# Output projection of a hybrid diffusion layer: the split of the activations moves one instruction ahead on ScalarE, and the last-but-one tile is normalised on VectorE

## The chip, the cores and the metric

The program runs on one core of a Trainium2 chip. The metric is the device time of one execution in microseconds (us). Engines are named as in the profile: PE is TensorE (PEld its weight loads), DVE is VectorE, ACT is ScalarE, POOL is GpSimd, and SP is the queue from which this kernel issues its transfers.

## The reference, cut to what matters

The kernel computes one layer for 2048 latent tokens and 128 context tokens. Three branches (a gated convolution, a gated spatial unit, windowed attention) give a concatenated activation of 1024 channels for each token. The change lies behind that, in the output projection and the closing normalisation:

```
out = jnp.concatenate([ya, yb, yc], axis=-1) @ w_out_l
x_new = _layernorm(ALPHA * x + gate[:, None] * out) * ln_g_l + ln_b_l
```

`_layernorm` subtracts the mean over the 1024 channels and divides by the root of the variance plus 1e-5.

## The kernel before

The branches write their activations, channels first, into a DRAM scratch `y_d`. The last stage reads them back in 17 tiles of 128 tokens (16 of the latent tokens, then the one of the context tokens) and runs one loop over these tiles, `for i in range(NT)`. There is no planner in this stage: every engine takes its instructions in the order in which the code is written.

For a tile, the following happens.

- SP loads the activations of the tile into `yf` (`out_load`, 512 KB, two buffers) and the residual input into `xr` (`x_again`, three buffers).
- The activations are split into a rounded part and a rest: ACT copies `yf` to `yh[:, 0]` (L1128), DVE subtracts that from `yf` and writes `yh[:, 1]` (L1129). Both are in `out_split`. The weights were split in the same way earlier.
- PE makes the tile's 1024 output columns in two halves of 512, each in a PSUM tile `ps` (three buffers), with 24 matmuls a half: 8 blocks of 128 channels by 3 products (rounded by rounded, rounded by rest, rest by rounded). The tile's `yh` is the weight that is loaded, so of a tile's 48 matmuls the first two need only the copy, and the third needs the subtraction too.
- DVE takes each half out of PSUM: times the gate (L1322), plus ALPHA times the residual (L1323), statistics (L1325). Behind the second half come the joined statistics (L1327) and a chain of instructions on single columns, L1329 to L1342, which makes the reciprocal root. This text calls it the chain.
- ACT then normalises the tile in place (L1343), POOL multiplies by `gam` (L1344) and adds `bet` (L1345), and SP stores the tile one iteration later (L1352).

In the code, `out_split` of tile i+1 stands at the head of iteration i. On ACT, therefore, the copy of a tile follows the normalisation of the tile two before it; on DVE the subtraction of a tile follows the chain of the tile two before it. The last tile (context) is made in three pieces of 512, 256 and 256 columns, and its normalisation is shared out among ACT, POOL and DVE (L1332 to L1350).

Of the kernel before, what the change touches and what calls it, by code (L numbers as in the profile page):

```python
# [11 lines left out]
F32 = mybir.dt.float32  # L12
F32R = mybir.dt.float32r
# [3 lines left out]
AF = mybir.ActivationFunctionType  # L17
ALU = mybir.AluOpType
# [4 lines left out]
P = 128  # L23
# [5 lines left out]
NT = TOK // P  # L29
# [67 lines left out]
    out_split=3100.0,  # L97
# [38 lines left out]
def hybrid_step(ctx: ExitStack, tc: tile.TileContext, x_prompt, x_sample, cache_k, cache_v, c, c_ctx,  # L136
# [3 lines left out]
    V, S, G, PE, SP = nc.vector, nc.scalar, nc.gpsimd, nc.tensor, nc.sync  # L140

    def open_pool(name, bufs=1, **kw):
        g = tc.tile_pool(name=name, bufs=bufs, **kw)
        return g, g.__enter__()
# [179 lines left out]
    for ks in VH:  # L324
        SP.dma_start(out=wB["v"]["st"][:, ks],
                     in_=w_in[0, ks.start * P:ks.stop * P, V0:V0 + 256].rearrange("(k p) f -> p k f", p=P))
# [16 lines left out]
    for g in range(4):  # L343
        SP.dma_start(out=bsb[64 * (g % 2):64 * (g % 2) + 64, g // 2, :],
                     in_=b_sp[0, g:g + 1, :].broadcast_to([64, P]))
# [774 lines left out]
    yhs, xts = {}, {}  # L1120

    def out_load(i):
        yhs[i] = outp["op"].tile([P, 8, P], F32, name="yf", bufs=2)
        SP.dma_start(out=yhs[i], in_=y_d[:, :, i * P:(i + 1) * P].rearrange("f p t -> p f t"))

    def out_split(i, yh):
        yf = yhs[i]
        S.activation(out=yh[:, 0], in_=yf, func=AF.Copy)  # L1128
        V.tensor_tensor(out=yh[:, 1], in0=yf, in1=yh[:, 0].bitcast(F32), op=ALU.subtract)  # L1129
        yhs[i] = yh  # L1130
# [20 lines left out]
    while cidx < len(jobs):  # L1151
# [37 lines left out]
        for ti, (t0, n) in enumerate(TILES):  # L1189
# [19 lines left out]
            if kind == "q":  # L1209
                for u in range(4 * ti, min(4 * ti + 4, 17)):  # L1210
# [4 lines left out]
                                       in1=QS[0:64, 0, t0:t0 + n], op0=ALU.mult, op1=ALU.subtract)  # L1215
                V.scalar_tensor_tensor(out=QS[0:64, 1, t0:t0 + n], in0=ps[64:128], scalar=cq[64:128],
                                       in1=QS[64:128, 1, t0:t0 + n], op0=ALU.mult, op1=ALU.subtract)
            elif kind == "k":
                for h in range(2):
# [3 lines left out]
                                           op0=ALU.mult, op1=ALU.subtract)  # L1223
                rng = {1: (0, 1024), 3: (1024, 2048)}.get(ti)
                if ti == 0:
                    cps = aps.tile([P, P], F32, name="cps", tag="o")
                    PE.transpose(cps, ckt, ident)
                    for h in range(2):
# [3 lines left out]
                                               op0=ALU.mult, op1=ALU.subtract)  # L1232
# [13 lines left out]
                if rng:  # L1246
                    r = slice(*rng)
# [37 lines left out]
    og2, o2 = open_pool("outl", side="left")  # L1285

    def x_again(i):
        xts[i] = o2.tile([P, D], F32, name="xr", bufs=3)
        SP.dma_start(out=xts[i], in_=src_rows(i))

    x_again(0)
    gam = o2.tile([P, D], F32, name="gam")
    bet = o2.tile([P, D], F32, name="bet")
# [5 lines left out]
    SP.dma_start(out=gam, in_=ln_g[0:1, :].broadcast_to([P, D]))  # L1299
    SP.dma_start(out=bet, in_=ln_b[0:1, :].broadcast_to([P, D]))  # L1300
    rs = {}
    for i in range(NT):
        if i + 1 < NT:
            out_split(i + 1, o2.tile([P, 2, 8, P], F32R, name="yh", bufs=2))
            x_again(i + 1)
        if i + 2 < NT:
            out_load(i + 2)
        yh, xt = yhs.pop(i), xts.pop(i)
        r = o2.tile([P, D], F32, name="r", bufs=3)
        last = i == NT - 1  # L1310
        cuts, sw = ((0, 512, 768, D), 256) if last else ((0, 512, D), 512)
        st = o2.tile([P, 8, 6], F32, name="ost", bufs=2)
        gt = gts[0 if i < NT - 1 else 1]
        for f0, f1 in zip(cuts, cuts[1:]):
            ps = aps.tile([P, 512], F32, name="ps", tag="pj", bufs=PJ)
            ps = ps[:, :f1 - f0]
            for k in range(KB):
                for q, (a, b) in enumerate(((0, 0), (0, 1), (1, 0))):
                    PE.matmul(out=ps, lhsT=yh[:, a, k, :], rhs=wo[:, b, k, f0:f1],  # L1319
                              start=(k == 0 and q == 0), stop=(k == KB - 1 and q == 2))  # L1320
            a = slice(f0, f1)
            V.tensor_tensor(out=r[:, a], in0=ps, in1=gt[:, a], op=ALU.mult)  # L1322
            V.scalar_tensor_tensor(out=r[:, a], in0=xt[:, a], scalar=ALPHA, in1=r[:, a], op0=ALU.mult, op1=ALU.add)  # L1323
            for b in range(f0, f1, sw):
                V.bn_stats(out=st[:, b // sw, :], in_=r[:, b:b + sw])  # L1325
        mv = o2.tile([P, 6], F32, name="omv", bufs=2)
        V.bn_aggr(out=mv[:, 0:2], in_=st[:, 0:D // sw])  # L1327
        v, y, t = mv[:, 1:2], mv[:, 2:3], mv[:, 3:4]
        V.tensor_scalar(out=v, in0=v, scalar1=EPS, scalar2=None, op0=ALU.add)  # L1329
        if last:  # L1330
            cut, mid = T["cut"], T["mid"]
            V.tensor_scalar(out=mv[:, 4:5], in0=mv[:, 0:1], scalar1=-1.0, scalar2=None, op0=ALU.mult)  # L1332
            S.activation(out=r[:, cut:], in_=r[:, cut:], func=AF.Identity, bias=mv[:, 4:5])
            G.tensor_tensor(out=r[:, cut:], in0=r[:, cut:], in1=gam[:, cut:], op=ALU.mult)
        V.tensor_scalar(out=t.bitcast(I32), in0=v.bitcast(I32), scalar1=1, scalar2=None, op0=ALU.logical_shift_right)  # L1335
        V.tensor_scalar(out=y.bitcast(I32), in0=t.bitcast(I32), scalar1=-1, scalar2=0x5F3759DF, op0=ALU.mult, op1=ALU.add)  # L1336
        for three in (3.0, 12.0, 768.0):
            V.scalar_tensor_tensor(out=t, in0=y, scalar=v, in1=y, op0=ALU.mult, op1=ALU.mult)  # L1338
            V.scalar_tensor_tensor(out=y, in0=t, scalar=three, in1=y, op0=ALU.subtract, op1=ALU.mult)  # L1339
        V.tensor_scalar(out=y, in0=y, scalar1=-1.0 / 8192, scalar2=None, op0=ALU.mult)  # L1340
        if not last:
            V.tensor_scalar(out=mv[:, 4:5], in0=mv[:, 0:1], scalar1=y, scalar2=-1.0, op0=ALU.mult, op1=ALU.mult)  # L1342
            S.activation(out=r, in_=r, func=AF.Identity, scale=y, bias=mv[:, 4:5])  # L1343
            G.tensor_tensor(out=r, in0=r, in1=gam, op=ALU.mult)  # L1344
            G.tensor_tensor(out=r, in0=r, in1=bet, op=ALU.add)  # L1345
        else:
            S.activation(out=r[:, mid:], in_=r[:, mid:], func=AF.Copy, scale=y)
            G.tensor_tensor(out=r[:, mid:], in0=r[:, mid:], in1=bet[:, mid:], op=ALU.add)
            V.scalar_tensor_tensor(out=r[:, :cut], in0=r[:, :cut], scalar=mv[:, 0:1], in1=gam[:, :cut], op0=ALU.subtract, op1=ALU.mult)  # L1349
            V.scalar_tensor_tensor(out=r[:, :mid], in0=r[:, :mid], scalar=y, in1=bet[:, :mid], op0=ALU.mult, op1=ALU.add)  # L1350
        if i > 0:
            SP.dma_start(out=y_sample[0, (i - 1) * P:i * P, :], in_=rs.pop(i - 1))  # L1352
        rs[i] = r
    r = rs.pop(NT - 1)
# [35 lines left out]
```

## Time and profile before

| | |
|---|---|
| median of 3 runs | 1187.61 us (1185.17 to 1192.42) |
| profiled execution, its own time | 1188.24 us |
| its span, first to last instruction | 1186.2 us |
| PE busy | 1069.7 us (90%) |
| DVE busy | 843.5 us (71%) |
| ACT busy | 447.3 us (38%) |
| POOL busy | 346.2 us (29%) |
| the last stage, from its first matmul to the end of the span | 958.6 to 1186.2 us |

The profiled execution lies 0.6 us above the median, so sums made against its 1188.24 us can be read against the median as they stand. 2.04 us of it lie outside the span. Shares of busy time are means over the whole program; what bounds the last stage is read from that stage alone.

### The profile page before, as it was taken

To read this page: it belongs to the slowest core of one execution; us is meant where nothing else is said; L and a number is where in the kernel's file an instruction comes from. 1 tells how busy PE (TensorE), PEld (TensorE's weight loads), DVE (VectorE), ACT (ScalarE), POOL (GpSimd) and SP (SyncE) were. 2 spreads that over 40 slices of the span, in tenths; PEclk is the share of its full clock that TensorE was granted. 3 is DMA by queue.
4 is the path that set the end of the run, shared out by engine and by line. 5 is a ranking of instruction groups with operands and counts; after the bars stand their busy time and mean duration, and the time that the engine had idled before them with its cause. 6 is when DMAs were issued, how large, how long until landed. Compare 5 with 4: busy or idle time off the path is not lost. (4 is left out here: it accounts for less than half of the span.)

```text
span 1186.2 us, 21036 instructions
## 1 busy us (share of the span) xinstructions
PE 1069.7 (90%) x8044; PEld 681.4 (57%) x8044; DVE 843.5 (71%) x2071; ACT 447.3 (38%) x758; POOL 346.2 (29%) x346
## 2 busy tenths in 40 slices
PE   5588989889968999999999999999988999888885
PEld 1377866477754455554545445545544477776774
DVE  4678866665562389954898549973899658777877
ACT  1432322223332266543655436753666321121111
POOL 0145655200002122102662022300325414334434
PEclk9699999989988999999999999999999999999998
DMA  9713104168957238754666746757476663433341
GB/s 330 260 43 103 59 10 142 54 211 294 308 185 197 77 74 147 130 127 102 113 145 122 152 105 125 150 125 150 97 136 119 198 211 107 144 123 106 120 129 54
DMA packets 254356, 165.50 MB, mean 140 GB/s; under 512 B 163600, under 2 KB 224808, under 8 KB 254256
## 3 DMA queue, kind: packets, MB, share of 16 engines
q1 hardware_dynamic: 254256, 164.16, 53.6%
q8 instruction: 63, 1.03, 0.4%
q14 instruction: 37, 0.30, 0.1%
HBM read 88.06 MB, written 36.21 MB: 105 GB/s over the span
## 5 line engine op out<-in xcount | busy, mean ns | idle before, releaser
L548 PE MATMUL pj<-h_hi,wring 128*128 128x512 f16 (+1 forms) x1280 | 336.2, 349 | 9.2 <-DMA wring<-wj_d 9.2
L548 PEld LDWEIGHTS <-wring 128*128 128x128 f16 x2400 | 211.7, 98 | 224.1 <-DMA wring<-wj_d 9.3
L548 PE MATMUL pj<-h_lo,wring 128*128 128x512 f16 (+1 forms) x640 | 217.9, 349 | 0.0
L1319 PE MATMUL ps<-wo,yh 128*128 128x512 f32 (+1 forms) x840 | 193.5, 390 | 21.0 <-DVE yh L1129 21.0
L1319 PEld LDWEIGHTS ps<-wo,yh 128*128 128x128 f32 x840 | 153.8, 188 | 60.5 <-DVE yh L1129 27.0
L1062 DVE SCALAR_TENSOR_TENSOR PH<-pt,sm,PH 128x608 f16<-128x608 f32 (+3 forms) x136 | 155.3, 1142 | 2.6 <-ACT PH L1059 2.4
L1002 POOL TENSOR_TENSOR TB<-raw,msk 128x480 f32<-128x480 f32 (+2 forms) x96 | 96.2, 1010 | 187.6 <-DVE sm L1043 187.6
L1059 ACT ACTIVATE PH<-pt,sm 128x608 f16<-128x608 f32 (+3 forms) x136 | 99.9, 734 | 95.1 <-ACT pt L1052 62.3
L1052 ACT ACTIVATE pt<-pt,sm,scal 128x608 f32<-128x608 f32 (+2 forms) x128 | 108.3, 846 | 57.6 <-DVE sm L1048 54.0
L1043 DVE CUSTOM_DVE_ANT_0 pt<-s,TB 128x608 f32<-128x608 f32 (+2 forms) x128 | 93.3, 729 | 11.2 <-PE s L1031 10.0
L558 PE MATMUL vvps<-wV,h_hi 128*128 128x256 f16 x544 | 94.0, 277 | 3.6 <-DVE vt L923 3.6
L558 PEld LDWEIGHTS <-h_hi 128*128 128x128 f16 x816 | 82.0, 102 | 23.1 <-issue 11.1
L548 PE MATMUL p<-h_hi,wring 128*128 128x512 f16 (+1 forms) x320 | 85.9, 352 | 1.9 <-DVE th L565 1.9
L1343 ACT ACTIVATE r<-r,omv 128x1024 f32<-128x1024 f32 x16 | 19.9, 1244 | 177.0 <-issue 141.1
L548 PEld LDWEIGHTS <-wB 128*128 128x128 f16 x768 | 63.4, 98 | 24.7 <-issue 1.3
L558 PE MATMUL vvps<-wV,h_lo 128*128 128x256 f16 x272 | 75.3, 277 | 0.0
L1344 POOL TENSOR_TENSOR r<-r,gam 128x1024 f32<-128x1024 f32 x16 | 38.2, 2388 | 126.4 <-ACT r L1343 126.4
L548 PE MATMUL ups<-h_hi,wB 128*128 128x128 f16 (+2 forms) x448 | 70.8, 267 | 0.3 <-DVE wB L238 0.3
L986 POOL TENSOR_SCALAR raw<-raw,scal 128x528 f32<-128x528 f32 x8 | 5.5, 704 | 220.2 <-DVE scal L189 165.8
L1129 DVE TENSOR_TENSOR yh<-yf,yh 128x1024 fp32r<-128x1024 f32 x17 | 41.0, 2410 | 35.2 <-ACT yh L1128 35.2
L1222 DVE SCALAR_TENSOR_TENSOR KL<-pj,scal,KH 64x512 f16<-64x512 f32 (+1 forms) x40 | 26.8, 670 | 54.1 <-ACT KH L1221 53.9
L496 POOL TENSOR_TENSOR h_lo<-hf,h_hi 128x512 f16<-128x512 f32 x34 | 39.9, 1179 | 74.9 <-DMA bsb<-in_b_spatial_dram 42.2
(214 smaller groups left out, 1712.0 us busy)
## 6 DMA issues: line engine op xcount, KB each, us to landing
wa<-in_w_ada_dram SPq DMA_DIRECT2D x24, 512.0 KB, 7.4
wraw<-in_w_in_dram SPq DMA_DIRECT2D x20, 512.0 KB, 5.7
wj_d<-wsp SPq DMA_DIRECT2D x40, 256.0 KB, 6.3
wring<-wj_d SPq DMA_DIRECT2D x20, 512.0 KB, 5.7
yf<-y_d SPq DMA_DIRECT2D x17, 512.0 KB, 5.6
xt<-in_x_sample_dram SPq DMA_DIRECT2D x16, 512.0 KB, 5.0
VW<-v_d SPq DMA_DIRECT2D x64, 128.0 KB, 5.1
xr<-in_x_sample_dram SPq DMA_DIRECT2D x16, 512.0 KB, 4.1
```

Of the source, the lines that this page charges most:

```text
L496: G.tensor_tensor(out=h_lo[:, k0:k0 + g, t0:t0 + n], in0=hv, in1=hi, op=ALU.subtract)
L548: PE.matmul(out=ps, lhsT=w(a, k) if callable(w) else w[:, a, k, :], rhs=mov(b, k), start=(k == 0 and i == 0), stop=(k == KB - 1 and i == 2))
L558: PE.matmul(out=ps, lhsT=a[:, k, i * P:(i + 1) * P], rhs=w[:, b, k, :], start=(k == 0 and q == 0), stop=(k == KB - 1 and q == 2))
L1002: G.tensor_tensor(out=TB[:, tslot(u) + h, P:P + n], in0=raws[h][:, off:off + n], in1=msk[:, mo:mo + n], op=ALU.add)
L1043: V.tensor_tensor_reduce(out=pt[:, :w], in0=src, in1=TB[:, tslot(u) + h, 0:w], op0=ALU.add, op1=ALU.max, scale=1.0, scalar=-3e38, accum_ou ...
L1052: S.activation(out=pt[:, :w], in_=src, func=AF.Exp, bias=sm[:, 1:2], scale=st_["isig"], accum_out=sm[:, 2:3])
L1059: S.activation(out=pb[:, 0:w], in_=pt[:, :w], func=AF.Copy, scale=sm[:, 3:4])
L1062: V.scalar_tensor_tensor(out=pb[:, wp:wp + w], in0=pt[:, :w], scalar=sm[:, 3:4], in1=pb[:, 0:w], op0=ALU.mult, op1=ALU.subtract)
L1129: V.tensor_tensor(out=yh[:, 1], in0=yf, in1=yh[:, 0].bitcast(F32), op=ALU.subtract)
L1222: V.scalar_tensor_tensor(out=KL[a, h, t0:t0 + n], in0=ps[a], scalar=ckk[a], in1=KH[a, h, t0:t0 + n], op0=ALU.mult, op1=ALU.subtract)
L1319: PE.matmul(out=ps, lhsT=yh[:, a, k, :], rhs=wo[:, b, k, f0:f1], start=(k == 0 and q == 0), stop=(k == KB - 1 and q == 2))
L1344: G.tensor_tensor(out=r, in0=r, in1=gam, op=ALU.mult)
```

## The change

Four things are done.

- `out_split` no longer runs inside the loop. Its two instructions become `yh_copy` and `yh_sub`. In iteration i, the copy of tile i+2 is issued on ACT ahead of the normalisation of tile i, and the subtraction of tile i+2 on DVE behind the chain of tile i.
- `yh` gets three buffers in place of two.
- The load of the activations is issued behind the subtraction, three tiles ahead, and so stands on SP in front of the store in place of behind it.
- Tile 15 (the last-but-one) is normalised by two DVE instructions of 1024 columns, in place of L1342, the ACT pass and the two POOL passes.

```
     rs = {}
+
+    def yh_copy(i):
+        if i < NT:
+            yh = o2.tile([P, 2, 8, P], F32R, name="yh", bufs=3)
+            S.activation(out=yh[:, 0], in_=yhs[i], func=AF.Copy)
+            yhs[i] = yhs[i], yh
+
+    def yh_sub(i):
+        if i < NT:
+            yf, yh = yhs[i]
+            V.tensor_tensor(out=yh[:, 1], in0=yf, in1=yh[:, 0].bitcast(F32), op=ALU.subtract)
+            yhs[i] = yh
+        if i + 1 < NT:
+            out_load(i + 1)
+
+    yh_copy(1)
+    yh_sub(1)
     for i in range(NT):
         if i + 1 < NT:
-            out_split(i + 1, o2.tile([P, 2, 8, P], F32R, name="yh", bufs=2))
             x_again(i + 1)
-        if i + 2 < NT:
-            out_load(i + 2)
         yh, xt = yhs.pop(i), xts.pop(i)
...
             a = slice(f0, f1)
+            if f0 == 0:
+                yh_copy(i + 2)
             V.tensor_tensor(out=r[:, a], in0=ps, in1=gt[:, a], op=ALU.mult)
...
-        if not last:
+        if i == NT - 2:
+            V.scalar_tensor_tensor(out=r, in0=r, scalar=mv[:, 0:1], in1=gam, op0=ALU.subtract, op1=ALU.mult)
+            V.scalar_tensor_tensor(out=r, in0=r, scalar=y, in1=bet, op0=ALU.mult, op1=ALU.add)
+        elif not last:
...
+        yh_sub(i + 2)
         if i > 0:
             SP.dma_start(out=y_sample[0, (i - 1) * P:i * P, :], in_=rs.pop(i - 1))
```

On ACT, early in the loop, the kernel before issues these (`r_11543`, `r_11625` and `r_11707` are tiles 1 to 3 under normalisation; `yh_11536` to `yh_11782` the split tiles 2 to 5):

```order
L1128 ACTIVATE yh_11536<-yf_11460 128x1024
L1343 ACTIVATE r_11543<-r_11543,omv_11601 128x1024
L1128 ACTIVATE yh_11618<-yf_11541 128x1024
L1343 ACTIVATE r_11625<-r_11625,omv_11683 128x1024
L1128 ACTIVATE yh_11700<-yf_11623 128x1024
L1343 ACTIVATE r_11707<-r_11707,omv_11765 128x1024
L1128 ACTIVATE yh_11782<-yf_11705 128x1024
```

The changed kernel issues these there (the same three tiles `r`; `yh_11489` to `yh_11734` are tiles 2 to 5):

```order
L1306 ACTIVATE yh_11489<-yf_11458 128x1024
L1362 ACTIVATE r_11462<-r_11462,omv_11522 128x1024
L1306 ACTIVATE yh_11570<-yf_11539 128x1024
L1362 ACTIVATE r_11543<-r_11543,omv_11603 128x1024
L1306 ACTIVATE yh_11652<-yf_11620 128x1024
L1362 ACTIVATE r_11625<-r_11625,omv_11685 128x1024
L1306 ACTIVATE yh_11734<-yf_11702 128x1024
L1362 ACTIVATE r_11707<-r_11707,omv_11767 128x1024
```

The copy of tile 5 stood behind the normalisation of tile 3 (`r_11707`) and now stands in front of it.

On DVE, at the boundary behind the chain of tile 3, the kernel before issues these (`omv` holds the single columns of the chain, `yh_11782` is tile 5, `r_11789` tile 4):

```order
L1340 TENSOR_SCALAR omv_11765<-omv_11765 128x1
L1342 TENSOR_SCALAR omv_11765<-omv_11765 128x1
L1129 TENSOR_TENSOR yh_11782<-yf_11705,yh_11782 128x1024
L1322 TENSOR_TENSOR r_11789<-ps_11791,gt0_11449 128x512
L1323 SCALAR_TENSOR_TENSOR r_11789<-xr_11703,r_11789 128x512
```

The changed kernel issues these there (`yh_11734` is tile 5):

```order
L1356 TENSOR_SCALAR omv_11767<-omv_11767 128x1
L1361 TENSOR_SCALAR omv_11767<-omv_11767 128x1
L1312 TENSOR_TENSOR yh_11734<-yf_11702,yh_11734 128x1024
L1338 TENSOR_TENSOR r_11789<-ps_11791,gt0_11449 128x512
L1339 SCALAR_TENSOR_TENSOR r_11789<-xr_11705,r_11789 128x512
```

Nothing moved on DVE here: the subtraction of tile 5 stood behind the chain of tile 3 already, since the head of one iteration and the end of the iteration before it are the same place.

At the end of the program DVE issues these in the changed kernel, behind the chain of tile 15 (`r_12689`) and ahead of the last tile (`r_12762`):

```order
L1356 TENSOR_SCALAR omv_12747<-omv_12747 128x1
L1358 SCALAR_TENSOR_TENSOR r_12689<-r_12689,omv_12747,gam_11447 128x1024
L1359 SCALAR_TENSOR_TENSOR r_12689<-r_12689,omv_12747,bet_11448 128x1024
L1338 TENSOR_TENSOR r_12762<-ps_12764,gt1_11451 128x512
L1339 SCALAR_TENSOR_TENSOR r_12762<-xr_12687,r_12762 128x512
```

The two instructions on 1024 columns are new on DVE; in the kernel before L1342 stood in their place.

## Rows read from the trace of the kernel before

**Rows 1.** The page: the span, and busy time, share of the span and instructions of PE and DVE.

```profile
span 1186.2 us, 21036 instructions
PE 1069.7 (90%) x8044; PEld 681.4 (57%) x8044; DVE 843.5 (71%) x2071; ACT 447.3 (38%) x758; POOL 346.2 (29%) x346
```

**Rows 2.** The waits from 990 to 1162 us: who waited for whom, us in total, times, the longest.

```profile
DVE yh L1129 <- ACT yh L1128: 32.2, 14, 2.3
PEld ps L1319 <- DVE yh L1129: 27.0, 14, 2.1
```

**Rows 3.** Weight loads of the last stage in order of time: start, length from the first to the last load of a run, count, and the idle time before the run with its releaser. The runs left out are like the third.

```profile
958.55 33.54 PEld L1319 LDWEIGHTS ps<-wo,yh 128*128 128x128 f32 x146
992.46 10.99 PEld L1319 LDWEIGHTS ps<-wo,yh 128*128 128x128 f32 x48 [0.37 <-DVE yh L1129]
...
1018.50 10.99 PEld L1319 LDWEIGHTS ps<-wo,yh 128*128 128x128 f32 x48 [2.05 <-DVE yh L1129]
1031.55 11.00 PEld L1319 LDWEIGHTS ps<-wo,yh 128*128 128x128 f32 x48 [2.06 <-DVE yh L1129]
...
1161.99 10.87 PEld L1319 LDWEIGHTS ps<-wo,yh 128*128 128x128 f32 x70 [2.05 <-DVE yh L1129]
```

**Rows 4.** Busy time of the engines in stretches of the last stage: the unbroken start, one tile of the steady part, the end.

```profile
core 0: us, PE busy (x) PEld busy (x) DVE busy (x) ACT busy (x) POOL busy (x), PEclk, DMA share, GB/s
958.50:991.50 33.00, 33.00 (x148) 26.94 (x146) 20.77 (x43) 5.70 (x6) 8.91 (x5) 1.00 0.62 201
1018.50:1031.55 13.05, 11.43 (x48) 8.96 (x49) 10.19 (x20) 2.19 (x2) 5.64 (x3) 1.00 0.38 122
1161.99:1186.20 24.21, 11.08 (x70) 9.90 (x70) 19.64 (x42) 2.54 (x3) 9.13 (x5) 0.79 0.17 66
```

**Rows 5.** One iteration of DVE in order of time, from the end of the chain of tile 3 to the subtraction of tile 6: start, length, instruction, idle time before it. The twelve instructions left out are L1322 of the second half of tile 4 and the chain of tile 4.

```profile
1013.37 0.21 DVE L1342 TENSOR_SCALAR omv<-omv 128x1 f32<-128x1 f32 x1
1015.89 2.56 DVE L1129 TENSOR_TENSOR yh<-yf,yh 128x1024 fp32r<-128x1024 f32 x1 [2.31 <-ACT yh L1128]
1018.37 0.68 DVE L1322 TENSOR_TENSOR r<-ps,gt 128x512 f32<-128x512 f32 x1
1019.08 2.17 DVE L1323 SCALAR_TENSOR_TENSOR r<-xr,r 128x512 f32<-128x512 f32 x1
1021.28 0.69 DVE L1325 BATCH_NORM_STATS2 ost<-r 128x6 f32<-128x512 f32 x1
...
1022.60 0.69 DVE L1323 SCALAR_TENSOR_TENSOR r<-xr,r 128x512 f32<-128x512 f32 x1
1023.33 0.69 DVE L1325 BATCH_NORM_STATS2 ost<-r 128x6 f32<-128x512 f32 x1
...
1026.41 0.21 DVE L1342 TENSOR_SCALAR omv<-omv 128x1 f32<-128x1 f32 x1
1028.93 2.57 DVE L1129 TENSOR_TENSOR yh<-yf,yh 128x1024 fp32r<-128x1024 f32 x1 [2.31 <-ACT yh L1128]
```

**Rows 6.** ACT, POOL and SP in the same iteration, in order of time.

```profile
1013.66 1.24 ACT L1343 ACTIVATE r<-r,omv 128x1024 f32<-128x1024 f32 x1 [10.86 <-issue]
1014.81 1.04 ACT L1128 ACTIVATE yh<-yf 128x1024 fp32r<-128x1024 f32 x1
1014.99 2.38 POOL L1344 TENSOR_TENSOR r<-r,gam 128x1024 f32<-128x1024 f32 x1 [7.33 <-ACT r L1343]
1017.44 3.25 POOL L1345 TENSOR_TENSOR r<-r,bet 128x1024 f32<-128x1024 f32 x1
1020.72 0.34 SPq L1352 DMA_DIRECT2D out_dram<-r  x1
1021.11 0.42 SPq L1289 DMA_DIRECT2D xr<-in_x_sample_dram  x1
1021.64 0.73 SPq L1124 DMA_DIRECT2D yf<-y_d  x1
```

**Rows 7.** The subtraction of tile 1, at the start of the stage, when POOL has no instruction running.

```profile
960.35 1.23 DVE L1129 TENSOR_TENSOR yh<-yf,yh 128x1024 fp32r<-128x1024 f32 x1 [0.15 <-ACT yh L1128]
```

**Rows 8.** The loads of `yf` from issue to landing, over the stage.

```profile
DMA to landing us min/median/max: 5.5/5.6/5.7
```

**Rows 9.** The end of the program on PE, POOL, DVE and SP: the last matmuls, the POOL passes of tile 15, the last two pieces of the last tile on DVE, the joined statistics, two instructions behind them, and the last store.

```profile
1161.99 11.08 PE L1319 MATMUL ps<-wo,yh 128*128 128x512 f32 x70 [1.61 <-DVE yh L1129]
1171.51 2.38 POOL L1344 TENSOR_TENSOR r<-r,gam 128x1024 f32<-128x1024 f32 x1 [7.32 <-ACT r L1343]
1172.13 0.41 DVE L1322 TENSOR_TENSOR r<-ps,gt 128x256 f32<-128x256 f32 x1
1172.57 1.60 DVE L1323 SCALAR_TENSOR_TENSOR r<-xr,r 128x256 f32<-128x256 f32 x1
1173.97 2.40 POOL L1345 TENSOR_TENSOR r<-r,bet 128x1024 f32<-128x1024 f32 x1
1174.20 0.43 DVE L1325 BATCH_NORM_STATS2 ost<-r 128x6 f32<-128x256 f32 x1
1174.55 0.41 DVE L1322 TENSOR_TENSOR r<-ps,gt 128x256 f32<-128x256 f32 x1
1174.99 1.66 DVE L1323 SCALAR_TENSOR_TENSOR r<-xr,r 128x256 f32<-128x256 f32 x1
1177.15 0.27 DVE L1327 BATCH_NORM_AGGREGATE omv<-ost 128x2 f32<-128x24 f32 x1
1178.71 1.20 DVE L1339 SCALAR_TENSOR_TENSOR omv<-omv 128x1 f32<-128x1 f32 x1
1182.88 0.33 SPq L1356 DMA_DIRECT2D out_dram<-r  x1
```

## The prediction

> **What bounds the kernel now.** The page comes first, and it says only where not to stop: PE is busy 90% of the span and DVE 71% [rows 1], means over stages with different limits. The change touches the last stage alone, so I went on to the list of waits for the steady part of that stage. The reader is to see two lines that belong together [rows 2]: PE's weight loads waited 14 times, 27.0 us in all, for the subtraction on DVE, and that subtraction waited 14 times, 32.2 us in all, for the copy on ACT. So PE waits for DVE and DVE for ACT, in every tile.
>
> How large is the wait per tile? The weight loads in order of time tell it [rows 3]. The stage begins with an unbroken run, 146 loads in 33.54 us, or 0.2297 us each; 48 of them, a tile, are 11.03 us. In the steady part a tile starts every 13.05 us (1018.50, 1031.55), with 2.05 us of idle time in front. So 13.05 - 11.03 = 2.02 us a tile are lost.
>
> Why does the copy come late? One iteration of DVE shows it [rows 5]: L1342 ends at 1013.58, then 2.31 us of idle time, then the subtraction. ACT in the same iteration [rows 6] starts the normalisation at 1013.66, just behind L1342, and the copy only behind that, at 1014.81. The copy's input is old by then; it waits for its place in ACT's queue. And the subtraction, when it comes, is held: it takes 2.56 us, while the one at the start of the stage takes 1.23 [rows 7]. POOL's first pass began at 1014.99, and 1014.99 + 2.38 = 1017.37; the subtraction ends 1.08 us behind that, so it began in earnest when POOL was done. The same happens to L1323, 2.17 us against 0.69 for its twin in the second half [rows 5], beside POOL's second pass [rows 6]. L1322 and the statistics, which overlap POOL as well (1174.20 and 1174.55 in rows 9), keep their length: it is instructions with two SBUF inputs that are held.
>
> The Trainium skill (SBUF — State Buffer, section SBUF: two separate sides) says that a VectorE instruction with two SBUF inputs and a GpSimd instruction need the same pair of ports, and that the later one fully blocks until the first has ended. The trace agrees, at 1.3 and 1.5 us a time.
>
> DVE's loop therefore is 13.04 us (1015.89 to 1028.93): 2.31 idle, 1.33 and 1.48 held, and 7.92 us of work that no one holds. DVE's loop, with that idle time in it, sets the pace, and PE follows with its own 11.03 us.
>
> **The change, part by part.** *The copy in front of the normalisation.* Count from the first matmul of tile i. PE is done with it at 11.0 us, DVE takes the second half and runs the chain (about 2.1 + 2.6 us) and reaches the end of it at 15.7. The copy of tile i+2 now needs three things: its input, a free `yh` buffer, and ACT. ACT's previous work, the normalisation of tile i-1, ends at about 15.7 - 11.03 + 1.3 = 6.0. The buffer is that of tile i-1, which PE left at 0. The input is loaded behind the subtraction of tile i, which ends at about -5; with 0.73 us of issue [rows 6] and 5.6 us to landing [rows 8] it is there at about 1.3. So the copy runs from 6.0 to 7.0, 8.7 us before DVE asks for it. The 2.31 us of idle time go altogether. What is queued behind the copy on ACT is the normalisation of tile i, which waits for the chain's end at 15.7 anyway.
>
> *The subtraction behind the chain.* It keeps its place on DVE. But it now starts when the chain ends, at 15.75, and ends 1.23 us later at 17.0, while POOL cannot start before ACT's 1.24 us are over (the first pass began 1.33 us behind the normalisation's start [rows 6]), at 17.1. So the hold of 1.33 us goes too. L1323 of the next first half then meets the first pass in place of the second, and I keep its 1.48. The second pass, delayed by that L1323, ends at about 22.2, just when L1323 of the second half can start; nothing or a few tenths.
>
> DVE's loop is then 7.92 + 1.48 = 9.4 us, below PE's 11.03. Even with today's holds, 10.73, it would be below. PE becomes the bound, and what is late next is PE itself, at 11.03 us a tile. Tile 16's operand needs the chain of tile 14 and is ready 4 to 5 us ahead.
>
> First term: thirteen tiles (4 to 16) at 2.02 us are 26.3, and tile 3 loses 0.37 now [rows 3], at most 0.3 of it beyond the normal spacing: **26.6 us**.
>
> *The third buffer and the load.* A third `yh` costs nothing that I can name; two would do, since the buffer of tile i is free at 11.0 and DVE asks at 15.7. On SP the load now stands ahead of the store. It waits for a subtraction that ends some 5 us before the POOL pass for which the store waits, so it delays no store. The residual load behind the store keeps its place. I take 0, with 0 to 1 us for a first wait when the larger pool opens.
>
> *Tile 15 on DVE.* In the kernel before, tile 15's two POOL passes run beside the last tile [rows 9]: 1.60 and 1.66 us for L1323 on 256 columns, where L1322 of the same width takes 0.41. PE ends at 1161.99 + 11.08 = 1173.07 and the joined statistics start at 1177.15, 4.08 us later. Without POOL, the last piece needs 0.41 + 0.41 + 0.43 us and three gaps, 1.5 us. Is DVE free in time? Counted from PE's third matmul of tile 16: the chain of tile 15 ends at about 4.4. No row shows the two new instructions; from below two inputs of 1024 columns cost 1.23 each [rows 7], from above 2.57, as a held one [rows 5]. I take 1.23, since POOL's last pass (tile 14) is over by 0.3: 6.9. First piece 2.2 us, second 1.3: 10.4, below PE's 11.08. At 2.57 each it would be 13.1, and the gain 0.6 in place of 2.6. Second term: **2.6 us** (0.6 to 2.6). Behind the joined statistics nothing changes; there one single-column L1339 is held too, 1.20 us, by the last tile's own POOL pass, and stays.
>
> The Trainium skill (Perfetto Trace Analysis, section Optimizing Scalar/DVE Operations) speaks against this last edit: since the two engines share a read port, moving work between them might not help. By that the second term would be 0, and the time 1161.6. The held rows of the trace say otherwise, because here the two engines' work is not just moved but put one behind the other.
>
> **The sum.** 1188.24 - 26.6 - 2.6 = **1159.0 us**. The profiled execution lies 0.6 us above the median of the three runs, so this stands against 1187.61 as it is: 2.4% less.
>
> **The rivals.** *POOL's holds keep DVE the bound.* DVE's loop exceeds PE's 11.03 when more than 11.03 - 7.92 = 3.1 us a tile are held. Two passes of 2.38 us can hold at most 4.8, so the loop is at most 12.7 and the time at most 1159.0 + 13 x 1.65 = 1180.5. For it: the single columns of the chain can be held too [rows 9], and the passes come at other moments now. Against it: all of today's holds are 2.8. In its middle, 11.85 us a tile, it gives 1169.7.
>
> *The change doesn't do what it says.* If the subtraction waited for something other than the copy's place in ACT's queue (the landing, the buffer), the loop would stay and only the second term would come: 1185.6. Against it: the copy starts within the very microsecond in which the normalisation ends, in every tile [rows 6].
>
> *Slower: the load becomes a loop.* The load of a tile waits for the subtraction of the tile two before, then lands, is copied and subtracted: (0.7 + L + 1.0 + 1.2) / 2 a tile, for a landing time L. And ACT's normalisation, POOL and the store now queue behind that copy. From L = 19 us it would exceed PE's pace, from 23 us that of the kernel before; at 26 us, 14.45 us a tile, the time is 1188.2 - 2.6 + 13 x 1.4 = 1204. Against it: 5.5 to 5.7 us in every load of today [rows 8], and the DMA engines are busy 0.38 of the steady part [rows 4], which would become 0.45.
>
> TensorE's clock is no rival that I can price from here: over the 33 us in which PE never paused, the granted clock was 1.00, the 2.4 GHz level [rows 4].
>
> **How the numbers follow.** My forecast has 0.86, holds 0.09, no effect 0.03, the loop of loads 0.02. The likeliest gives 1159.0. Its own range is 1156 to 1163: the three runs of before lie 2.4 us under and 4.8 over their median, the second term may be 2 us short, the pool's opening 1 us. With a part of the first rival the range is 1155 to 1167. This kernel's measurement can tell about 1% from no change, 12 us. Faster by more: the forecast and two thirds of the first rival, 0.92. Within 1%: the rest of that, and no effect, 0.06. Slower: 0.02.
>
> **What the changed profile would show.** Right: PE's weight loads run on from 958.5 us to the end with no wait for the subtraction, a tile every 11.0 us; the copy on ACT starts some 8 us before its subtraction; the subtraction takes 1.23 us; DVE waits for PE at the second half of each tile; the joined statistics of the last tile start 1.5 us behind PE's end. Wrong: waits of PE for the subtraction of over 0.2 us a tile, an L1323 or chain instructions of over 1 us twice in a tile, or a copy that waits for a DMA.

## The result and the profile after

The changed kernel takes 1159.45 us (median of 4 runs, 1158.58 to 1161.21) against 1187.74 us before (4 runs, 1185.17 to 1192.42): a ratio of 0.9761, 95% interval 0.9736 to 0.9786. The profiled execution took 1161.21 us, with a span of 1159.1 us. The forecast was 1159.0 us.

The page after, where it answers [rows 1], and the first line of its chain that ended last:

```profile
span 1159.1 us, 21031 instructions
PE 1067.3 (92%) x8044; PEld 683.9 (59%) x8044; DVE 829.0 (72%) x2072; ACT 446.2 (38%) x757; POOL 333.8 (29%) x344
...
PE 18%; DMA 2%; DVE 1%; ACT 0%; issue 0%; SPq 0%; DVEq 0%
```

PE's weight loads of the last stage in order of time, after, which answer [rows 3]: start, length from the first to the last load, count.

```profile
958.81 189.59 PEld L1333 LDWEIGHTS ps<-wo,yh 128*128 128x128 f32 x840
```

Where before there were fourteen runs of loads with an idle time in front of each but the first, there is one run of 840. PE never waits in this stage, and the chain of work that ended last now goes through PE.

The waits from 955 us to the end, after, which answer [rows 2] (who waited for whom, us in total, times, the longest):

```profile
DVE r L1338 <- PE ps L1333: 20.9, 17, 1.4
...
ACT yh L1306 <- DMA yf<-y_d: 14.6, 2, 13.8
...
DVE yh L1312 <- ACT yh L1306: 0.8, 2, 0.7
```

The relation is turned round: DVE waits for PE, 17 times, up to 1.4 us. The copy waits for a load twice, 13.8 and 0.8 us, both at the start of the stage (those loads were issued at 963.29 and 967.66 us among the stage's first transfers, and the two copies start at 974.38 and 977.40); DVE waits for the copy 0.8 us in all. In the steady part no copy waits for a load.

One iteration of DVE after, from the subtraction of one tile to that of the next, which answers [rows 5], and ACT and POOL beside it, which answer [rows 6]:

```profile
1019.34 1.22 DVE L1312 TENSOR_TENSOR yh<-yf,yh 128x1024 fp32r<-128x1024 f32 x1
1020.48 0.68 DVE L1338 TENSOR_TENSOR r<-ps,gt 128x512 f32<-128x512 f32 x1
1021.19 2.60 DVE L1339 SCALAR_TENSOR_TENSOR r<-xr,r 128x512 f32<-128x512 f32 x1
...
1025.84 0.69 DVE L1338 TENSOR_TENSOR r<-ps,gt 128x512 f32<-128x512 f32 x1 [1.32 <-PE ps L1333]
1026.57 0.69 DVE L1339 SCALAR_TENSOR_TENSOR r<-xr,r 128x512 f32<-128x512 f32 x1
...
1030.49 1.22 DVE L1312 TENSOR_TENSOR yh<-yf,yh 128x1024 fp32r<-128x1024 f32 x1
```

```profile
1019.51 1.25 ACT L1362 ACTIVATE r<-r,omv 128x1024 f32<-128x1024 f32 x1 [8.96 <-issue]
1020.66 1.04 ACT L1306 ACTIVATE yh<-yf 128x1024 fp32r<-128x1024 f32 x1
1020.83 2.40 POOL L1363 TENSOR_TENSOR r<-r,gam 128x1024 f32<-128x1024 f32 x1 [5.92 <-ACT r L1362]
1023.32 2.73 POOL L1364 TENSOR_TENSOR r<-r,bet 128x1024 f32<-128x1024 f32 x1
```

The loop is 11.15 us (1030.49 - 1019.34). The subtraction is no longer held: 1.22 us. It is over at 1020.56, just before POOL's first pass begins at 1020.83. L1339 of the first half meets that pass and ends 0.56 us behind it, 1.91 us longer than its twin at 1026.57. The copy that ends at 1021.70 is for the subtraction at 1030.49: it is 8.8 us early.

Where the time went, stage by stage, from the two profiled executions:

| | before | after | difference |
|---|---|---|---|
| start of the program to the first weight load of the stage | 958.55 | 958.81 | +0.26 |
| first weight load to the end of the last matmul | 214.52 | 189.80 | -24.7 |
| end of the last matmul to the joined statistics of the last tile | 4.08 | 1.49 | -2.6 |
| joined statistics to the end of the span | 9.01 | 9.00 | 0.0 |

The end of the last matmul and the joined statistics after, for the table; the row of PE runs from its window's start, and 1114.63 + 33.98 is the end:

```profile
1114.63 33.98 PE L1333 MATMUL ps<-wo,yh 128*128 128x512 f32 x169
...
1150.10 0.26 DVE L1343 BATCH_NORM_AGGREGATE omv<-ost 128x2 f32<-128x24 f32 x1
```

One thing has to be known for all the medians below. The code ahead of the last stage is the same in nearly all these kernels, and yet the stage's first weight load came between 953.4 and 958.9 us in their profiles. Two profiles of the changed kernel itself have it at 958.81 and at 955.22, with the stage 200.3 us long in both. Differences of 2 or 3 us between medians are of that size; for these, the length of the stage in the trace, first weight load to the end of the span, is the better measure: 227.6 us before, 200.3 us after. The ratio and interval given with a time are to the kernel before, timed in the same rounds.

### The profile page after: what moved, and what is told of

Same layout as the page of the kernel before. It is cut to its first block, busy times and chain, and to the rows that moved or that the text cites. A ratio compares the mean times of both kernels' runs of the same rounds, so it can differ in the third digit from the quotient of the medians.

```text
span 1159.1 us, 21031 instructions
## 1 busy us (share of the span) xinstructions
PE 1067.3 (92%) x8044; PEld 683.9 (59%) x8044; DVE 829.0 (72%) x2072; ACT 446.2 (38%) x757; POOL 333.8 (29%) x344
## 5 line engine op out<-in xcount | busy, mean ns | idle before, releaser
L1333 PE MATMUL ps<-wo,yh 128*128 128x512 f32 (+1 forms) x840 | 189.8, 388 | 0.0
L548 PEld LDWEIGHTS <-wB 128*128 128x128 f16 x768 | 63.4, 98 | 24.7 <-issue 1.3
L487 ACT ACTIVATE hf<-tp,modT 128x128 f32<-128x128 f32 (+2 forms) x64 | 33.6, 577 | 67.3 <-PE tp L475 41.6
```

Of the source, the lines that this page charges most:

```text
L487: S.activation(out=hf[:, a], in_=tp[:, a], func=AF.Identity, scale=modT[:, 8 + k, m:m + 1], bias=modT[:, k, m:m + 1])
L548: PE.matmul(out=ps, lhsT=w(a, k) if callable(w) else w[:, a, k, :], rhs=mov(b, k), start=(k == 0 and i == 0), stop=(k == KB - 1 and i == 2))
```

## The experiments

**The copy behind the normalisation again.** The changed kernel with one thing undone.

```
-            if f0 == 0:
-                yh_copy(i + 2)
...
+        yh_copy(i + 2)
         yh_sub(i + 2)
```

> The changed kernel with one thing undone: the copy of tile i+2 is issued on ACT behind the normalisation of tile i again; third buffer, early load and the tail stay. Theory (the copy's place in ACT's queue made the wait): DVE's loop is 13.0 us a tile again, PE waits some 1.9 us in each of 13 tiles, only the tail's 2.6 us stay: 1185 us. Rival (the third buffer or the earlier load gave the gain): 1159 to 1160 us.

Measured: 1187.21 us (ratio to before 1.0003, 0.9981 to 1.0026). Its weight loads in order of time, two runs of the steady part:

```profile
1016.41 11.00 PEld L1333 LDWEIGHTS ps<-wo,yh 128*128 128x128 f32 x48 [2.02 <-DVE yh L1312]
1029.45 10.99 PEld L1333 LDWEIGHTS ps<-wo,yh 128*128 128x128 f32 x48 [2.05 <-DVE yh L1312]
```

A tile every 13.04 us, and 2 us of idle time in front: the loop of before. So in this kernel the whole gain hangs on the place of that one instruction on ACT. The expectation was 2 us off: the tail's gain did not stay either (3.94 us from the last matmul to the joined statistics, 4.08 before). The experiments on the copy's order alone, on tile 15 alone and on the old tail go after that.

**The copy's order alone.** The kernel before with the copy in front: two buffers of `yh`, the load behind the store, POOL's work on tile 15 as before. The lines are against the changed kernel; its `out_load` in `yh_sub` and its branch for tile 15 are taken out too.

```
...
-    yh = o2.tile([P, 2, 8, P], F32R, name="yh", bufs=3)
+    yh = o2.tile([P, 2, 8, P], F32R, name="yh", bufs=2)
...
+        if i + 2 < NT:
+            out_load(i + 2)
```

> The kernel before with one thing changed: on ACT the copy of tile i+2 stands in front of the normalisation of tile i. Two yh buffers, the load behind the store and POOL's normalisation of tile 15 are as before. Theory: PE is the bound at 11.15 us a tile; all of the gain but the tail's 2.6 us: 1162 us. Rival (it needs the third buffer or the early load too): the copy still comes late, 1170 to 1185 us.

Measured: 1160.91 us (0.9781, 0.9751 to 0.9811), the stage 201.0 us. Its weight loads, and a wait that is new (990 to 1130 us):

```profile
958.35 189.59 PEld L1333 LDWEIGHTS ps<-wo,yh 128*128 128x128 f32 x840
```

```profile
ACT yh L1306 <- PE ps L1333: 66.8, 13, 5.2
```

One run of 840 loads, of the same 189.59 us. With two buffers ACT waits 5.2 us a tile for PE to leave one, and that costs nothing. Where DVE begins the last tile, in the kernel before and then here, and here also PE's end (1129.74 + 18.40 = 1148.14; the row runs from its window's start) and the joined statistics:

```profile
1170.02 0.68 DVE L1322 TENSOR_TENSOR r<-ps,gt 128x512 f32<-128x512 f32 x1
```

```profile
1129.74 18.40 PE L1333 MATMUL ps<-wo,yh 128*128 128x512 f32 x102
...
1142.55 0.69 DVE L1338 TENSOR_TENSOR r<-ps,gt 128x512 f32<-128x512 f32 x1 [0.90 <-PE ps L1333]
...
1150.33 0.26 DVE L1343 BATCH_NORM_AGGREGATE omv<-ost 128x2 f32<-128x24 f32 x1
```

Before, DVE began that tile 3.1 us before PE's end (1173.07) and without a wait; now it begins it 5.6 us before PE's end and waits for PE. The joined statistics start 2.2 us behind the last matmul: so the order of the copy alone brings 1.9 of the 2.6 us that the prediction had booked under the tail's edit.

**Tile 15 on DVE alone.** The kernel before with the two DVE instructions in place of ACT's and POOL's work on tile 15.

```
-        if not last:
+        if i == NT - 2:
+            V.scalar_tensor_tensor(out=r, in0=r, scalar=mv[:, 0:1], in1=gam, op0=ALU.subtract, op1=ALU.mult)
+            V.scalar_tensor_tensor(out=r, in0=r, scalar=y, in1=bet, op0=ALU.mult, op1=ALU.add)
+        elif not last:
```

> The kernel before with tile 15 normalised by two DVE instructions in place of ACT and POOL, nothing else. Theory: the last pieces of the last tile are no longer held, but the chain of tile 15 and the last pieces come when they came: 2.6 us less than before, 1185 us. Rival (the Trainium skill's rule, in which work moved between the two engines gains nothing): 1187.7 us.

Measured: 1184.66 us, 0.9983 with an interval of 0.9961 to 1.0005, which holds no change, and the median 3 us below before: by itself that decides nothing. The trace does. PE and DVE at its end:

```profile
1156.85 11.08 PE L1319 MATMUL ps<-wo,yh 128*128 128x512 f32 x70 [1.61 <-DVE yh L1129]
```

```profile
1164.63 1.27 DVE L1342 SCALAR_TENSOR_TENSOR r<-r,omv,gam 128x1024 f32<-128x1024 f32 x1
1165.94 1.28 DVE L1343 SCALAR_TENSOR_TENSOR r<-r,omv,bet 128x1024 f32<-128x1024 f32 x1
1167.15 0.68 DVE L1322 TENSOR_TENSOR r<-ps,gt 128x512 f32<-128x512 f32 x1
...
1169.70 0.42 DVE L1323 SCALAR_TENSOR_TENSOR r<-xr,r 128x256 f32<-128x256 f32 x1
...
1170.95 0.43 DVE L1323 SCALAR_TENSOR_TENSOR r<-xr,r 128x256 f32<-128x256 f32 x1
...
1171.87 0.26 DVE L1327 BATCH_NORM_AGGREGATE omv<-ost 128x2 f32<-128x24 f32 x1
```

The holds of [rows 9] are gone: 0.42 and 0.43 us where there were 1.60 and 1.66. But the two new instructions cost 2.5 us, and DVE begins the last tile's first piece at 1167.15, 0.8 us before PE ends the whole tile (1156.85 + 11.08 = 1167.93). DVE is behind, so what it saves in holds it spends again, and the joined statistics start 3.94 us behind PE in place of 4.08. The stage is 227.5 us long against 227.6, and began 5.2 us earlier (953.36): the lower median is no gain of the edit. Alone, the edit brings 0.1 us.

**Two buffers of the split tile.** The changed kernel with `bufs=2` for `yh`.

> The changed kernel with two yh buffers in place of three. Theory: the copy of tile i+2 must wait until PE has left tile i, 11 us after its start, and DVE asks for it at 15.8: no change, 1159.5 us. Rival (the third buffer carries part of the gain): PE waits again, 1165 us or more.

Measured: 1160.8 us (0.9778, 0.9749 to 0.9807), the stage 200.4 us against 200.3. The third buffer carries nothing that the trace shows.

**Without POOL's passes.** The kernel before, copy behind the normalisation, and L1344 and L1345 taken out, so that tiles 0 to 15 are not scaled by `gam` nor shifted by `bet`.

```
-            G.tensor_tensor(out=r, in0=r, in1=gam, op=ALU.mult)
-            G.tensor_tensor(out=r, in0=r, in1=bet, op=ALU.add)
```

> The kernel before without POOL's two passes over tiles 0 to 15 (their gam and bet are left out, so that part of the result is not computed); the copy stays behind the normalisation. Theory (the lateness is the sum of the queue's 2.31 us and POOL's holds of 2.8 us a tile): DVE's loop is 7.92 + 2.31 = 10.2 us, below PE's 11.15, PE stops waiting and the tail is not held: 1159 to 1161 us. Rival (the copy's place alone decides): PE waits on, 1180 to 1185 us.

Measured: 1154.28 us (0.973, 0.9704 to 0.9756). DVE and the weight loads:

```profile
1016.32 1.23 DVE L1129 TENSOR_TENSOR yh<-yf,yh 128x1024 fp32r<-128x1024 f32 x1 [2.26 <-ACT yh L1128]
```

```profile
953.44 189.60 PEld L1319 LDWEIGHTS ps<-wo,yh 128*128 128x128 f32 x840
```

DVE still idles 2.26 us in front of every subtraction, as before, and PE does not wait at all. So the wait of before had two parents, the queue on ACT (2.31 us) and the holds beside POOL (2.8 us), and taking away either brings DVE's loop below PE's. The median lies 5 us under what was expected; the stage is 200.2 us long, just that of the changed kernel, and it began 5 us earlier, so that is no gain of this stage.

**One subtraction more.** The changed kernel with the subtraction issued twice.

```
             V.tensor_tensor(out=yh[:, 1], in0=yf, in1=yh[:, 0].bitcast(F32), op=ALU.subtract)
+            V.tensor_tensor(out=yh[:, 1], in0=yf, in1=yh[:, 0].bitcast(F32), op=ALU.subtract)
```

> The changed kernel with each subtraction in the loop issued twice (1.22 us more of DVE a tile, the same result). Theory: DVE's loop, 9.8 us with its holds in the trace of the changed kernel, becomes about 10.9 to 11.05, still below PE's 11.15: 1159.5 to 1161 us. Rival (DVE has no room left, or POOL's holds grow with it): 1.2 us a tile more, 1175 us.

Measured: 1162.61 us (0.9797, 0.9779 to 0.9815). Late in the stage PE waits a little, and on DVE L1340 (L1339 of the changed kernel) is held in both halves of a tile, by POOL's first pass and by its second:

```profile
1124.20 10.99 PEld L1334 LDWEIGHTS ps<-wo,yh 128*128 128x128 f32 x48 [0.35 <-DVE yh L1313]
```

```profile
1102.11 2.17 DVE L1340 SCALAR_TENSOR_TENSOR r<-xr,r 128x512 f32<-128x512 f32 x1
...
1105.63 1.45 DVE L1340 SCALAR_TENSOR_TENSOR r<-xr,r 128x512 f32<-128x512 f32 x1
```

DVE's loop is 11.33 us, 0.18 over PE's. The subtraction alone, 1.22 us, would have fitted into the 1.32 us that DVE idled in a tile; but the holds grew with it, from 1.91 us a tile to 1.48 and 0.76. That is the expectation's rival, at 0.18 us a tile and not at 1.2. The median lies 1.6 us over the upper end of the expectation. In the trace the stage is 204.7 us long, 4.4 over the changed kernel's: 0.8 of it are PE's waits, 3.3 DVE, now behind at the last tile, where the joined statistics start 4.8 us behind PE's end, and 0.4 lie behind those.

**Two subtractions more.** The same with three.

> The changed kernel with each subtraction in the loop issued three times (2.44 us more of DVE a tile). Theory: DVE's loop of 12.1 to 12.3 us passes PE's 11.15, and PE waits 0.9 to 1.1 us in some 13 tiles: 1171 to 1174 us. Rival (PE does not hang on DVE's loop any more): 1160 us; rival (no room in DVE at all): 1191 us.

Measured: 1200.87 us (1.0111, 1.0088 to 1.0135), slower than before and far over what was expected. DVE and POOL in one iteration, and two runs of weight loads:

```profile
1067.39 1.22 DVE L1312 TENSOR_TENSOR yh<-yf,yh 128x1024 fp32r<-128x1024 f32 x1
1068.64 1.23 DVE L1313 TENSOR_TENSOR yh<-yf,yh 128x1024 fp32r<-128x1024 f32 x1
1068.88 3.24 POOL L1365 TENSOR_TENSOR r<-r,gam 128x1024 f32<-128x1024 f32 x1 [7.32 <-ACT r L1364]
1069.90 3.31 DVE L1314 TENSOR_TENSOR yh<-yf,yh 128x1024 fp32r<-128x1024 f32 x1
1072.20 3.26 POOL L1366 TENSOR_TENSOR r<-r,bet 128x1024 f32<-128x1024 f32 x1
1073.84 2.17 DVE L1341 SCALAR_TENSOR_TENSOR r<-xr,r 128x512 f32<-128x512 f32 x1
```

```profile
1003.86 10.98 PEld L1335 LDWEIGHTS ps<-wo,yh 128*128 128x128 f32 x48 [2.88 <-DVE yh L1314]
1017.74 10.99 PEld L1335 LDWEIGHTS ps<-wo,yh 128*128 128x128 f32 x48 [2.90 <-DVE yh L1314]
```

The third subtraction finds POOL's first pass in its way and takes 3.31 us, 2.1 of them held; L1341 then meets the second pass, 1.5 held. 7.92 + 2.5 + 2.1 + 1.5 = 14.0, against a tile every 13.88 us. The expectation had counted the instructions and kept the holds as they were; they grow from 1.9 to 3.6 us a tile. It is the prediction's first rival at work, in a kernel made for it: both passes hold DVE, 2.1 and 1.5 us. The passes themselves are longer here too, 3.24 and 3.26 us in place of 2.40 and 2.73.

**One buffer for the loaded tile.** The changed kernel with `bufs=1` for `yf`.

> The changed kernel with one yf buffer in place of two, so that the load of tile i+3 waits for the subtraction of tile i+2 and the store behind it on SP waits too. Theory: the load lands some 5 us behind that subtraction, the copy is done some 4 us before DVE asks for it: no change, 1159.5 us. Rival (the loop of loads is near): PE waits 1 us a tile or more, 1172 us or more.

Measured: 1160.88 us (0.9779, 0.9761 to 0.9798), the stage 200.3 us. The copy now waits for the load in every tile (990 to 1130 us), and nobody waits for the copy:

```profile
ACT yh L1306 <- DMA yf<-y_d: 59.8, 13, 5.2
```

The loop of loads, the slower rival, is far off even so.

**The old tail in the changed kernel.** Tile 15 goes back to ACT and POOL.

```
-        if i == NT - 2:
...
-        elif not last:
+        if not last:
```

> The changed kernel with tile 15 normalised by ACT and POOL again, nothing else. Theory (with PE as the bound, DVE is no longer behind when the last tile comes; only the holds beside POOL's passes of tile 15 are left): the joined statistics of the last tile start 2.2 us behind PE's end in place of 1.5, 0.7 us more, 1160 us. Rival (the two DVE instructions carry the whole second term of the prediction): 2.6 us more, 1162 us.

Measured: 1159.33 us (0.9772, 0.9746 to 0.9799). Its last pieces on DVE; PE ends at 1145.41:

```profile
1144.41 1.39 DVE L1339 SCALAR_TENSOR_TENSOR r<-xr,r 128x256 f32<-128x256 f32 x1
...
1146.62 0.43 DVE L1339 SCALAR_TENSOR_TENSOR r<-xr,r 128x256 f32<-128x256 f32 x1
...
1147.61 0.26 DVE L1343 BATCH_NORM_AGGREGATE omv<-ost 128x2 f32<-128x24 f32 x1
```

2.2 us from PE's end to the joined statistics, 0.7 more than in the changed kernel. That is what the edit of the tail is worth, too little for the medians to show.

**The split tiles beside tile 0's.** In the changed kernel tile 0's `yh` lies in the pool of the weights, that of all later tiles in another. In its trace tile 0's weight loads follow each other at 227 ns and those of all later tiles at 232 ns, and the change comes exactly with the first matmul of tile 1.

```
...
-            outp[k] = outp["op"].tile([P, D], F32, name="wos", bufs=3)
+            outp[k] = outp["op"].tile([P, D], F32, name="wos", bufs=2)
...
-            yh = o2.tile([P, 2, 8, P], F32R, name="yh", bufs=3)
+            yh = outp["op"].tile([P, 2, 8, P], F32R, name="yh", bufs=2)
```

> The changed kernel with the split tiles yh laid out in the pool that holds tile 0's (two buffers, one tag with tile 0's; to make room the staging of the output weights has two buffers in place of three). In the changed kernel the matmuls of tile 0 follow each other at 227 ns, those of all later tiles at 232 ns. Theory (where yh lies sets the spacing): 227 ns throughout, 792 matmuls on 512 columns less tile 0's 48, at 5 ns: the stage 3.7 us shorter, 1156 us. Rival (something else about tile 0 sets it): 232 ns from tile 1 on, 1159.5 us.

Measured: 1163.36 us (0.9792, 0.9773 to 0.9811). Its weight loads:

```profile
964.28 185.77 PEld L1333 LDWEIGHTS ps<-wo,yh 128*128 128x128 f32 x840
```

840 loads in 185.77 us in place of 189.59, as expected. The time was not: the stage began at 964.28, 5.5 us later than in the changed kernel and later than in any other profile here. With two staging buffers the copies of the output weights waited 16.2 us for their loads in place of 9.8. So the room was taken elsewhere.

**The same, with one `yf` buffer.** The staging keeps its three buffers, `yf` has one.

> The changed kernel with the split tiles yh in the pool that holds tile 0's, as before, but the room now made by one yf buffer in place of two; the staging of the output weights keeps its three buffers. Theory (where yh lies sets the spacing; one yf buffer costs nothing, the two staging buffers were what delayed the start of the stage): 227 ns throughout, 840 weight loads in 185.8 us in place of 189.6, and the stage starts as in the changed kernel: 3.8 us below that, some 1155.5 us. Rival (the spacing came with the two staging buffers, or the start of the stage moves with the pool): no gain over the changed kernel.

> The changed kernel itself, unchanged, timed in the same rounds as the kernel with yh moved: 1159.5 us by every theory.

Measured in the same rounds: 1156.55 us (0.9741, 0.9715 to 0.9767), and the changed kernel 1158.84 us (0.9765, 0.9739 to 0.979). The weight loads of the first:

```profile
958.86 185.38 PEld L1333 LDWEIGHTS ps<-wo,yh 128*128 128x128 f32 x840
```

And the weight loads that fall into the 135 us from 985 to 1120 us, in the changed kernel of these rounds and then in the one with `yh` moved (count, busy time, length of one in ns, idle time between them):

```profile
L1333 PEld LDWEIGHTS ps<-wo,yh 128*128 128x128 f32 x582 | 109.6, 188 | 25.6
```

```profile
L1333 PEld LDWEIGHTS ps<-wo,yh 128*128 128x128 f32 x597 | 112.0, 188 | 23.3
```

One load takes 188 ns in both; 135 us hold 582 of them there, 232 ns each, and 597 here, 226 ns each. The stage is 196.1 us long against 200.3, and starts at 958.86, within the spread named above. The median is 2.3 us lower; the two intervals overlap, so the timing alone would not prove it. The trace does for the stage: 4.2 us of 200, and it is the shortest stage of the kernels that compute the whole result.

## Why the prediction came out

*The bound.* Right. PE waited for DVE and DVE for ACT's queue; with the copy in front (the copy's order alone) all waits of PE go, with the copy behind they are all back. That the holds alone would not make PE wait was in the prediction's sum (7.92 + 2.8 = 10.7 us, below PE). That the queue alone would not either (7.92 + 2.31 = 10.2 us) was not in it; the kernel without POOL's passes shows it.

*The first term* was forecast at 26.6 us and measured 24.7. The mechanism was right, PE's own pace was mis-sized: 11.03 us a tile, where the changed kernel needs 11.15. The step that failed is the division of 33.54 us by 146 loads in [rows 3]. A third of that run is tile 0, whose loads come at 227 ns, and the run ends with a load, not with the space behind it. Tiles 1 and 2, in the same run of the kernel before, come at 232 ns a load and would have told it. So it is 13.05 - 11.15 = 1.90 us a tile, not 2.02.

*The second term* was forecast at 2.6 us and measured 2.6, but the cause was wrong. The step that failed is the booking of all of 4.08 - 1.5 us under the edit of tile 15, as if POOL's passes alone made the 4.08. Before, DVE came late to the last tile (3.1 us before PE's end). With PE as the bound DVE is in time, POOL's passes of tile 15 hold pieces that come earlier, and that alone brings 1.9 us; the two DVE instructions bring 0.7 then, and 0.1 without it. The Trainium skill's sentence that moving work between VectorE and GpSimd might not help (Perfetto Trace Analysis, section Optimizing Scalar/DVE Operations) was set aside in the prediction for the held rows. The kernel with that edit alone agrees with it, at 0.1 us; with PE as the bound the same edit gains 0.7.

*The holds.* The subtraction is free of POOL, as forecast. L1339 is held 1.91 us where 1.48 was carried over from before: it now arrives 0.36 us into a pass of 2.40 us. DVE's loop is 9.83 us of work and holds (11.15 less 1.32 idle), not 9.4. It cost nothing: 1.32 us a tile are left, which one subtraction more with the holds that it brings uses up.

*What was costed at nothing.* The third buffer and the load ahead of the store: right, by the kernel with two buffers (200.4 us of stage against 200.3) and by the copy's order alone, where the third buffer, the early load and the new tail are all missing and the stage is 201.0 us, just that of the changed kernel with the old tail. The prediction's 5.5 to 5.7 us "in every load of today" [rows 8] is a reading of two loads, the only ones of `yf` whose landing that trace has.

*The sum.* In the trace the gain is 27.3 us, not 29.2, less the 0.26 us by which the stage began later: the profiled execution took 1161.21 us, 2.2 over the forecast. That the median lies within 0.5 us of it is partly luck, since executions scatter by several us ahead of the stage.

*The signs.* Those named for right all came, with a tile every 11.15 us in place of 11.0. One named for wrong came too, a copy that waits for a DMA, but only for the first two copies of the loop, and PE did not wait for it.

*The rivals.* None came about. Two subtractions more show the first one's mechanism, with 3.6 us held a tile; that the third is far is shown by one `yf` buffer, with which the copy waits up to 5.2 us for its load and PE not at all.

## What to carry to other kernels

Look for the instruction whose input has long been there and which waits only for its place in a queue: one swap on ACT was worth 26.6 us of the stage here, and three other edits of the same change 0.7 us together. When an engine stops being late, what follows it at the end of the program gets better too; do not book that under an edit made there. And where DVE and POOL share a stage, added DVE work costs its own time and what it then collides with: 2.5 us of it cost 2.7 us of PE's time a tile, though 1.3 us of room was there.

## What the runs showed of the hardware that was not expected

The place in SBUF of the operand that is loaded as weights sets the pace of these matmuls. With `yh` in the one pool, 840 loads took 189.59 us, in the other 185.38 us, on the same instructions: about 232 and 227 ns each on 512 columns. Tile 0 in all traces shows it, and the two kernels with `yh` moved; it is not the number of buffers, since two in the old pool left the stage at 200.4 us, and not POOL's passes, since without them 840 loads still took 189.60 us. In the code the slower place is a pool opened with `side="left"`, the faster one a pool opened with `side="right"`, in which the weights `wo` lie too. What it is about the place, an address, a neighbour, or other tiles that moved with it, stays open.

The load of `yf` took 4.4 and 4.2 us to land in the changed kernel (4.9 and 3.8 in its second profile), against 5.7 and 5.5 before [rows 8]; each trace has the landing of two such loads. It is issued some 5 us behind the residual load now, where before it followed that in half a microsecond [rows 6]. In the copy's order alone, where it still follows that closely, it took 5.4 us. That the distance is the cause is not shown.
